# A decoder step on one core: output and gate-path weights split once into a DRAM copy, and fetched ready-made

## The chip, the core and the metric

The kernel runs on one core of a Trainium2 chip. The metric is the device time of one execution in microseconds (us). Five engines work side by side, each through its own instructions in a fixed order: the tensor engine (PE; its weight loads are listed apart as PEld), the vector engine (DVE), the scalar engine (ACT), GpSimd (POOL), and the sync engine (SP), which here only issues DMAs. An instruction that waits for a semaphore holds back all that stands behind it on its engine.

## What is computed

A layer of a hybrid decoder for 1024 prompt tokens and 8 single sample tokens with a cache. Cut to what matters here:

```python
q, ckv, skv, wkv, gl, za, u, zp = split(rmsnorm(x) @ w_in)
o_a = nsa_attention(q, gl, ckv, skv, wkv, ...)      # 3 branches, gated, 8 heads
o_p = pool_mixer(u, ...)                            # windows 2, 4, 8, 16
mix = concat([o_a * silu(za), o_p * silu(zp)])
y = rmsnorm(x + mix @ w_out)
```

The 512 columns `za` of `w_in` (the gate path of the attention group) and the 1024 x 1024 matrix `w_out` are the weights that the change is about.

## The kernel before, in words

Float32 products are made from float32r pieces: a matrix is split into a high part (`hi`, a rounded copy) and a low part (`lo`, the rest), and three matmuls (hi by hi, hi by lo, lo by hi) are summed. `split_w` (line 142) makes the pair from a raw tile: ACT copies, and DVE or GpSimd subtracts.

The stages in the order of the program: projection of the K/V columns; compression of the cache blocks and the `q` columns, with `q` written to DRAM (`q_d`); the pooling stage, a loop over 4 channel groups `g` (lines 798 to 856), each with a `u` and a `zp` weight tile through `load_tile` (line 387) and `feat_unit` (line 400), with the one-token attention `decode()` (line 548) woven between; then the prompt's attention in 32 units (query block `i`, head pair `j`, line 1148), and the end.

`decode()` has higher priority and works in a memory pool `dp`, which is closed at line 718. The pools that are opened after that on the same side (`at`, the attention's tiles) take over its addresses.

A unit of the attention has two halves. `stage1` (line 739) makes scores on PE (`S`, line 773, from a `qt` tile that `load_q` fetched from `q_d`), adds masks on DVE (line 736), takes the exponential on ACT (line 786) and scales on GpSimd (line 793), giving the tiles `Ps` and `Pw`. `stage2` (line 867) transposes those on PE (lines 883 and 891), splits them on ACT and DVE (lines 885 to 897) and multiplies by V (lines 902 to 909). `stage1` of the next unit runs among the steps of `stage2`.

Between the steps, `paced_fill` (line 1130) takes matmuls from a generator `filler` (line 1086). It gives first the `za` projection (`za_fill`, line 959: 4 weight tiles `pt` by 3 token chunks `c`, 24 matmuls each, lines 968 to 970), then the output projection (`out_half`, line 1069, matmuls at line 1042). `za_fill` loads and splits a weight tile with `load_tile`; after the last tile of each chunk it calls `load_wo(c)` (line 979), which puts split rows of `w_out` into the place of the input chunk that is no longer needed.

The framework's scheduler sets each engine's order at build time, by priority and by its own estimate of when an instruction is ready. Nothing is reordered on the chip.

Of the kernel before, what the change touches and what calls it, by code (L numbers as in the profile page):

```python
# [7 lines left out]
F32 = mybir.dt.float32  # L8
F32R = mybir.dt.float32r
I32 = mybir.dt.int32  # L10
BF16 = mybir.dt.bfloat16
AF = mybir.ActivationFunctionType
# [24 lines left out]
def r32(ap):  # L37
    return ap.bitcast(F32)
# [3 lines left out]
def hybrid_step_kernel(ctx, tc, xp, xs, ccmp, cslc, cwin, spool, ptab, norm_g, w_in, cmp_pe, cmp_w1,  # L42
# [17 lines left out]
    def ps_t(name="tp"):  # L60
        return psum.tile([128, 512], F32, name=name, tag="tp", bufs=3)
# [17 lines left out]
    b_d = dram.tile([4, 128, TOK], F32, name="b_d")  # L79
    g_d = dram.tile([NB, 24], F32, name="g_d")  # L80
    kc_d = dram.tile([2, 128, 128], F32, name="kc_d")


    ident = pers.tile([128, 128], F32, name="ident")
# [57 lines left out]
    def split_w(hi, lo, raw, eng=None):  # L142
        nc.scalar.activation(hi, raw, AF.Copy)
        (eng or nc.vector).tensor_sub(lo, raw, r32(hi))
# [252 lines left out]
    def w_cols(c0):  # L397
        return w_in.rearrange("(k p) c -> p k c", p=128)[:, :, c0:c0 + 128]
# [10 lines left out]
    def silu2(out, src):  # L409

        nc.scalar.activation(out, src, AF.Tanh, scale=0.5)
        nc.vector.scalar_tensor_tensor(out, out, 1.0, src, op0=OP.add, op1=OP.mult)
# [305 lines left out]
    des.close()  # L718


    at = ctx.enter_context(tc.tile_pool(name="at", bufs=2, reuse_waits="tile"))
    UNITS = [(i, j) for i in range(8) for j in range(4)]
    q_tiles = {}
    soft = {}
# [73 lines left out]
    for g in range(4):  # L798
        w = 2 << g
        hi, lo = load_tile(w_cols(C_U + g * 128))  # L800
        u = pu.tile([128, H0 + TOK], F32, name="u", bufs=2)
        nc.vector.memset(u[:, :H0], 0.0)
        for c in range(3):
            p, t0, n = feat_unit(hi, lo, c)
            nc.scalar.activation(u[:, H0 + t0:H0 + t0 + n], p[:, :n], AF.Copy)
        p = ps_t("ut")
        nc.tensor.transpose(p[:15, :128], u[:, H0 + T - 15:H0 + T], ident)
        nc.tensor.transpose(p[:NB, 128:256], u[:, H0 + T:H0 + TOK], ident)
        nc.tensor.transpose(p[:, 256:376], spt[:, g * 128:(g + 1) * 128], ident[:120, :120])
        nc.vector.tensor_copy(utok[:15, g * 128:(g + 1) * 128], p[:15, :128])  # L810
        nc.vector.tensor_copy(utoks[:, g * 128:(g + 1) * 128], p[:NB, 128:256])
        us = pp.tile([128, NB, 16], F32, name="us", bufs=2)
        nc.vector.tensor_copy(us[:, :, :15], p[:, 256:376].rearrange("p (b s) -> p b s", b=NB))
        nc.vector.tensor_copy(us[:, :, 15], u[:, H0 + T:H0 + TOK])
        cur = u
        step = 1
        k = 0
        while step < w:
            nx = pp.tile([128, H0 + TOK], F32, name=f"ws{k % 2}")
            nc.vector.memset(nx[:, :H0], 0.0)  # L820
            nc.vector.tensor_add(nx[:, H0:H0 + T], cur[:, H0:H0 + T], cur[:, H0 - step:H0 + T - step])
            cur = nx
            step *= 2
            k += 1
        nc.vector.tensor_reduce(cur[:, H0 + T:H0 + TOK], us[:, :, 16 - w:], axis=AX.X, op=OP.add)
        nc.vector.scalar_tensor_tensor(cur[:, H0:H0 + w - 1], cur[:, H0:H0 + w - 1], float(w),
                                       cnt[:, :w - 1], op0=OP.mult, op1=OP.mult)
        dd = cur[:, H0:]
        nc.vector.scalar_tensor_tensor(dd, dd, 1.0 / w, u[:, H0:], op0=OP.mult, op1=OP.subtract)
        if g == 2:  # L830
            load_q(0, 0)
            load_q(0, 1)
        if g == 3:
            for _ in stage1(*UNITS[0]):
                pass
        hi, lo = load_tile(w_cols(C_ZP + g * 128))
        sz = pu.tile([128, TOK], F32, name="sz")
        for c in range(3):
            p, t0, n = feat_unit(hi, lo, c)
            silu2(sz[:, t0:t0 + n], p[:, :n])  # L840
        if g:
            bb = pp.tile([128, TOK], F32, name="bb")
        for c in range(3):
            t0, n = CHUNKS[c]
            p = ps_t("yp")
            nc.tensor.matmul(p[:, :n], pw[:, g, :], dd[:, t0:t0 + n], start=True, stop=True)
            cs = slice(t0, t0 + n)
            if c < 2:
                nc.vector.scalar_tensor_tensor(bb[:, cs], p[:, :n], psc[:, g:g + 1], sz[:, cs],
                                               op0=OP.mult, op1=OP.mult)  # L850
            else:

                nc.scalar.activation(bb[:, cs], p[:, :n], AF.Copy, scale=psc[:, g:g + 1])
                nc.gpsimd.tensor_mul(bb[:, cs], bb[:, cs], sz[:, cs])
                nc.gpsimd.tensor_copy(bs_t[:, g, :], bb[:, T:])
        nc.gpsimd.dma_start(b_d[g], bb)
    tc.keep_in_program_order(nc.sync.dma_start(npool_p, utok[:15]))
    tc.keep_in_program_order(nc.sync.dma_start(npool_s[:, 14], utoks))
    pes.close()


# [97 lines left out]
    def za_fill():  # L959
        w = {}  # L960
        for pt, c in ZORD:
            if pt not in w:
                w[pt] = load_tile(w_cols(C_ZA + pt * 128))
            hi, lo = w[pt]
            for t0, n in CHUNKS[c:c + 1]:
                p = ps_j()
                for k in range(8):
                    nc.tensor.matmul(p[:, :n], hi[:, k, :], xh[c][:, k, :], start=k == 0, stop=False)  # L968
                    nc.tensor.matmul(p[:, :n], hi[:, k, :], xl[c][:, k, :], start=False, stop=False)  # L969
                    nc.tensor.matmul(p[:, :n], lo[:, k, :], xh[c][:, k, :], start=False, stop=k == 7)  # L970
                    if k == 7:
                        gate(pt, t0, n, p)
                    yield
            if pt == 3:
                with tc.high_priority(2000):
                    load_wo(c)
        xt_es.close()

    def load_wo(c):

        rows = WROWS[c]
        w = xtp.tile([128, 2, CHUNKS[c][1] * 8], F32R, name=f"wo{c}", tag=f"x{c}")
        w = w[:, :, :512 * len(rows)].rearrange("p f (k c) -> p f k c", c=512)
        for j in range(0, len(rows), 2):
            half, k = rows[j]
            raw = rp.tile([128, 2, 512], F32, name="wo_raw", tag="r")
            nc.sync.dma_start(raw, w_out[k * 128:(k + 2) * 128, half * 512:half * 512 + 512]
                              .rearrange("(k p) c -> p k c", p=128))
            for kk in range(2):
                nc.scalar.activation(w[:, 0, j + kk], raw[:, kk], AF.Copy)  # L990
                (nc.vector, nc.gpsimd)[kk].tensor_sub(w[:, 1, j + kk], raw[:, kk], r32(w[:, 0, j + kk]))
                O_[half, k + kk] = w[:, 0, j + kk], w[:, 1, j + kk]

    def open_out():
        fp, op = (ctx.enter_context(tc.tile_pool(name=n, bufs=1, side="right", reuse_waits="tile"))
# [275 lines left out]
```

## Time and profile before

| what | value |
|---|---|
| median of 3 runs | 641.39 us (641.33 to 641.68) |
| the profiled execution's own time | 641.35 us |
| its span, first to last instruction | 639.7 us |
| PE busy | 625.0 us, 4176 matmuls |
| PEld busy | 581.1 us |
| DVE busy | 420.9 us |
| ACT busy | 364.1 us |
| POOL busy | 270.2 us |
| share of the chain that ended last | PE 90%, DVE 4%, issue 2% |

The profiled execution takes 1.65 us more than its span, for what lies around the instructions. Busy time of PE counts modelled ends of pipelined matmuls, so small gaps can hide in it.

### The profile page before, as it was taken

How to read it: one execution, taken by the hardware profiler on the slowest of the kernel's cores; microseconds unless marked ns; L12 is line 12 of the kernel's file. 1: busy time of each engine (PE TensorE's matmuls, PEld its weight loads, DVE VectorE, ACT ScalarE, POOL GpSimd, SP SyncE). 2: the span in 40 equal slices, each digit the busy share in tenths (PEclk: the TensorE clock that was granted, in tenths of full speed). 3: DMA queues.
4: the chain of work that ended last, by engine and by line, in shares of the span. 5: the costliest groups of instructions: out<-in, count | busy, mean ns of one | idle time of the engine just before them, and what ended most of it. 6: DMA issues, size and time to landing. Idle time of an engine off the chain costs nothing.

```text
span 639.7 us, 12220 instructions
## 1 busy us (share of the span) xinstructions
PE 625.0 (98%) x4176; PEld 581.1 (91%) x4176; DVE 420.9 (66%) x1237; ACT 364.1 (57%) x931; POOL 270.2 (42%) x412
## 2 busy tenths in 40 slices
PE   8999999999999999999999999999999999999995
PEld 5999999999999899999899999788899999998895
DVE  6754234637264547466787999778888787877653
ACT  5654223536223333218787988767686767676742
POOL 6144004404035624006546767544545555444510
PEclk9999999999999999999999999999999999999998
DMA  8435107956234532243313456403113020101001
GB/s 281 151 91 156 34 1 223 287 199 193 61 80 135 158 98 87 84 119 93 91 34 99 121 189 184 118 18 100 37 50 98 17 100 17 67 17 67 17 34 66
DMA packets 63741, 65.13 MB, mean 102 GB/s; under 512 B 4487, under 2 KB 55119, under 8 KB 63639
## 3 DMA queue, kind: packets, MB, share of 16 engines
q1 hardware_dynamic: 53631, 44.55, 23.0%
q0 software_dynamic: 4000, 12.76, 6.3%
q10 hardware_dynamic: 6048, 7.05, 3.2%
q8 instruction: 33, 0.54, 0.3%
q14 instruction: 29, 0.24, 0.1%
HBM read 50.98 MB, written 15.68 MB: 104 GB/s over the span
## 4 chain that ended last, share of the span: by engine, by line
PE 90%; DVE 4%; issue 2%; DMA 1%; ACT 1%; POOL 1%; DVEq 0%; POOLq 0%; ACTq 0%
PE pj L1042 14%; PE S L773 9%; PE tp L891 8%; PE pa L404 7%; PE pa L405 7%; PE pa L406 7%; PE O L909 5%; PE O L908 4%; PE pa L277 4%; PE pa L275 3%; PE pa L276 3%; PE pj L968 2%; PE pj L969 2%; PE pj L970 2%; PE xtp_ps L230 1%
## 5 line engine op out<-in xcount | busy, mean ns | idle before, releaser
L793 POOL TENSOR_SCALAR Ps<-Ps,sm,gates 128x64 f32<-128x64 f32 (+1 forms) x120 | 76.4, 647 | 87.5 <-DVE sm L789 57.9
L897 DVE TENSOR_TENSOR pl<-tp,ph 128x512 fp32r<-128x512 f32 (+1 forms) x136 | 89.9, 670 | 21.2 <-ACT ph L896 19.9
L773 PE MATMUL S<-KT,qt 128*128 128x320 f32 (+10 forms) x400 | 99.5, 347 | 3.1 <-DVE sm L736 3.1
L896 ACT ACTIVATE ph<-tp 128x512 fp32r<-128x512 f32 (+1 forms) x136 | 77.1, 580 | 31.4 <-PE tp L891 21.5
L404 PE MATMUL pa<-x,ws_hi 128*128 128x384 f32 (+1 forms) x288 | 93.7, 325 | 0.0
L406 PE MATMUL pa<-x,ws_lo 128*128 128x384 f32 (+1 forms) x288 | 92.9, 323 | 0.0
L405 PE MATMUL pa<-x,ws_hi 128*128 128x384 f32 (+1 forms) x288 | 92.7, 322 | 0.0
L786 ACT ACTIVATE Ps<-Ps,sm 128x64 f32<-128x64 f32 (+8 forms) x128 | 71.0, 555 | 24.5 <-DVE sm L736 22.5
L1042 PE MATMUL pj<-wo,mh 128*128 128x512 f32 (+1 forms) x272 | 84.5, 385 | 0.0
L909 PE MATMUL O<-pl,V 128*128 128x256 f32 x264 | 76.5, 308 | 0.2
L908 PE MATMUL O<-ph,V 128*128 128x256 f32 x264 | 74.5, 298 | 0.0
L773 PEld LDWEIGHTS S<-KT,qt 128*128 128x128 f32 x400 | 63.2, 189 | 9.0 <-DVE sm L736 3.5
L1042 PEld LDWEIGHTS pj<-wo,mh 128*128 128x128 f32 x272 | 48.4, 188 | 6.9 <-DVE r L1054 0.3
L405 PEld LDWEIGHTS pa<-x,ws_hi 128*128 128x128 f32 x288 | 54.2, 188 | 0.4 <-issue 0.3
L404 PEld LDWEIGHTS pa<-x,ws_hi 128*128 128x128 f32 x288 | 54.2, 188 | 0.4
L406 PEld LDWEIGHTS pa<-x,ws_lo 128*128 128x128 f32 x288 | 54.2, 188 | 0.2
L277 PE MATMUL pa<-w_hi,x 128*128 128x256 f32 (+1 forms) x184 | 52.9, 288 | 1.2 <-DVE x L236 1.2
L275 PE MATMUL pa<-w_hi,x 128*128 128x256 f32 (+1 forms) x184 | 53.6, 292 | 0.0
L909 PEld LDWEIGHTS O<-pl,V 128*128 128x128 f32 x264 | 49.8, 189 | 2.9 <-DVE pl L897 0.6
L276 PE MATMUL pa<-w_lo,x 128*128 128x256 f32 (+1 forms) x184 | 52.4, 285 | 0.0
L1042 PE MATMUL pj<-wo,ml 128*128 128x512 f32 (+1 forms) x136 | 51.7, 380 | 0.0
L908 PEld LDWEIGHTS O<-ph,V 128*128 128x128 f32 x264 | 49.9, 189 | 1.8
(294 smaller groups left out, 1530.5 us busy)
## 6 DMA issues: line engine op xcount, KB each, us to landing
ws_raw<-in_w_in SPq DMA_DIRECT2D x32, 256.0 KB, 3.0
qt<-q_d SPq DMA_DIRECT2D x64, 128.0 KB, 2.9
x_t<-in_x_prompt SPq DMA_DIRECT2D x8, 512.0 KB
wo_raw<-in_w_out SPq DMA_DIRECT2D x8, 512.0 KB, 3.8
r<-in_x_prompt SPq DMA_DIRECT2D x8, 512.0 KB, 3.2
out<-r SPq DMA_DIRECT2D x7, 512.0 KB, 2.9
q_d<-qhl ACTq DMA_DIRECT2D x8, 384.0 KB, 3.9
out<-kvf ACTq DMA_DIRECT2D x5, 512.0 KB, 3.1
```

The lines of the kernel that those rows point to most:

```text
L275: nc.tensor.matmul(p[:n, :cn], xh[c][:, k, ts_], hi[:, k, :cn], start=k == 0, stop=False)
L277: nc.tensor.matmul(p[:n, :cn], xl[c][:, k, ts_], hi[:, k, :cn], start=False, stop=k == 7)
L404: nc.tensor.matmul(p[:, :n], hi[:, k, :], xh[c][:, k, :], start=k == 0, stop=False)
L405: nc.tensor.matmul(p[:, :n], hi[:, k, :], xl[c][:, k, :], start=False, stop=False)
L406: nc.tensor.matmul(p[:, :n], lo[:, k, :], xh[c][:, k, :], start=False, stop=k == 7)
L773: nc.tensor.matmul(S[:, :ln], qt[:, f, h, :], KT[:, kv, k0 + a:k0 + a + ln], start=f == 0, stop=f == 1)
L793: nc.gpsimd.tensor_scalar(regs[br], regs[br], sm[:, hh, 2, br:br + 1], gsrc[:, k:k + 1], op0=OP.mult, op1=OP.mult)
L896: nc.scalar.activation(ph[:, :m], tp[:, :m], AF.Copy)
L897: nc.vector.tensor_sub(pl[:, :m], tp[:, :m], r32(ph[:, :m]))
L908: nc.tensor.matmul(O[:, :256], vv, ph[:, a * 256:(a + 1) * 256], start=False, stop=False)
L909: nc.tensor.matmul(O[:, :256], vv, pl[:, a * 256:(a + 1) * 256], start=False, stop=last)
L1042: nc.tensor.matmul(p, a[:, k % 4, :], w, start=first and kk == 0, stop=last and kk == 2)
```

## The change

Two DRAM tensors are added: `zw_d` for the split gate-path weights and `wo_d` for the split output weights. The pooling loop now calls `stage_some(3)` at two places in each of its 4 rounds, which makes 24 tiles in all: 8 of gate-path weights and 16 of output weights. For one tile SP loads 256 KB into `sraw`, ACT copies the high part into half of `sw`, GpSimd subtracts into the other half, and a DMA from GpSimd's queue writes the 512 KB of `sw` to DRAM. `sraw` and `sw` have two buffers each, in a pool `stg` that is opened right behind `at`, in memory that `decode()` had. `za_fill` and `load_wo` then fetch the split tiles from SP's queue and no longer split anything.

```diff
+    zw_d = dram.tile([4, 2, 128, 1024], F32, name="zw_d")
+    wo_d = dram.tile([2, 8, 128, 2, 512], F32, name="wo_d")
...
+    ses = ExitStack()
+    to_stage = [(zw_d[pt, :, :, kk * 128:(kk + 4) * 128].rearrange("f p c -> p f c"),
+                 w_cols(C_ZA + pt * 128)[:, kk:kk + 4], 4) for pt in range(4) for kk in (0, 4)]
+    to_stage += [(wo_d[half, k], w_out[k * 128:(k + 1) * 128, half * 512:half * 512 + 512], 1)
+                 for rows in WROWS for half, k in rows]
+
+    def stage_some(n):
+        for dst, src, k in to_stage[:n]:
+            raw = stg.tile([128, 512], F32, name="sraw", bufs=2)
+            nc.sync.dma_start(raw.rearrange("p (k c) -> p k c", k=k) if k > 1 else raw, src)
+            w = stg.tile([128, 2, 512], F32R, name="sw", bufs=2)
+            split_w(w[:, 0], w[:, 1], raw, nc.gpsimd)
+            nc.gpsimd.dma_start(dst, r32(w))
+        del to_stage[:n]
+
     at = ctx.enter_context(tc.tile_pool(name="at", bufs=2, reuse_waits="tile"))
+    stg = ses.enter_context(tc.tile_pool(name="stg", bufs=1, reuse_waits="tile"))
...
             nc.scalar.activation(u[:, H0 + t0:H0 + t0 + n], p[:, :n], AF.Copy)
+        stage_some(3)
...
             silu2(sz[:, t0:t0 + n], p[:, :n])
+        stage_some(3)
...
+    ses.close()
     pes.close()
...
-                w[pt] = load_tile(w_cols(C_ZA + pt * 128))
+                w[pt] = [ws.tile([128, 8, 128], F32R, name=n, bufs=2) for n in ("ws_hi", "ws_lo")]
+                for f in range(2):
+                    nc.sync.dma_start(r32(w[pt][f].rearrange("p k c -> p (k c)")), zw_d[pt, f])
...
-        for j in range(0, len(rows), 2):
-            half, k = rows[j]
-            raw = rp.tile([128, 2, 512], F32, name="wo_raw", tag="r")
-            nc.sync.dma_start(raw, w_out[k * 128:(k + 2) * 128, half * 512:half * 512 + 512]
-                              .rearrange("(k p) c -> p k c", p=128))
-            for kk in range(2):
-                nc.scalar.activation(w[:, 0, j + kk], raw[:, kk], AF.Copy)
-                (nc.vector, nc.gpsimd)[kk].tensor_sub(w[:, 1, j + kk], raw[:, kk], r32(w[:, 0, j + kk]))
-                O_[half, k + kk] = w[:, 0, j + kk], w[:, 1, j + kk]
+        for j, (half, k) in enumerate(rows):
+            nc.sync.dma_start(r32(w[:, :, j]), wo_d[half, k])
+            O_[half, k] = w[:, 0, j], w[:, 1, j]
```

The order that the scheduler made of it is shown at three places. Lines in the rows of the changed kernel are its own: 143 has become 145, 411 is 413, 853 is 874, 786 is 805, 732 is 751.

On ACT, at the end of the pooling stage, there stood before (`sz` is the gate of the last group, `ws_hi` the first two copies for `za_fill`, `bb` the last pooling output, `Ps` and `Pw` the first exponentials of the attention):

```order
L411 ACTIVATE sz<-pa 128x384
L143 ACTIVATE ws_hi<-ws_raw 128x512 x2
L411 ACTIVATE sz<-pa 128x264
L853 ACTIVATE bb<-yp,psc 128x264
L786 ACTIVATE Ps,sm<-Ps,sm 128x64
L786 ACTIVATE Ps,sm<-Ps,sm 128x128
L786 ACTIVATE Pw,sm<-Pw,sm 128x128
```

and now:

```order
L413 ACTIVATE sz<-pa 128x384
L413 ACTIVATE sz<-pa 128x264
L145 ACTIVATE sw<-sraw 128x512 x2
L874 ACTIVATE bb<-yp,psc 128x264
L145 ACTIVATE sw<-sraw 128x512 x13
L805 ACTIVATE Ps,sm<-Ps,sm 128x64
L805 ACTIVATE Ps,sm<-Ps,sm 128x128
L805 ACTIVATE Pw,sm<-Pw,sm 128x128
```

The copies of 15 of the 24 tiles stand behind the last `sz` and ahead of the first exponential. From the third on, each waits in the built program for its own load and for the DMA that wrote the tile two before it. The first load of `sraw` waits for PE and GpSimd instructions of `decode()`.

Further on ACT, among the first units' exponentials, stand the other 9 copies (`pc` and `ph` are the first transposed blocks of the attention, `zt` the first gate of `za_fill`):

```order
L145 ACTIVATE sw<-sraw 128x512
L805 ACTIVATE Ps,sm<-Ps,sm 128x128
L805 ACTIVATE Pw,sm<-Pw,sm 128x128 x2
L145 ACTIVATE sw<-sraw 128x512 x6
L907 ACTIVATE pc<-tp 64x256
L918 ACTIVATE ph<-tp 128x512
L907 ACTIVATE pc<-tp 64x256
L145 ACTIVATE sw<-sraw 128x512
L962 ACTIVATE zt<-pj 128x384
```

GpSimd has the subtractions and writes in the same order: 15 ahead of its first scaling of the attention, the 16th after nine scalings, the 17th after three more, and after six more, which end the third unit, the last 7 in one piece ahead of the fourth unit's first scaling.

On SP, at the same point, the order was (`qt` are the query tiles of the attention, eight DMAs for the four pairs of one query block):

```order
L393 DMA ws_raw<-in_w_in 128x4x128 x12
L857 DMA out<-utok 15x512
L858 DMA out<-utok 8x512
L732 DMA qt<-q_d 64x4x128 x16
L393 DMA ws_raw<-in_w_in 128x4x128 x2
```

and is now:

```order
L732 DMA sraw<-in_w_in 128x4x128 x4
L987 DMA ws_hi<-zw_d 128x1024
L987 DMA ws_lo<-zw_d 128x1024
L732 DMA sraw<-in_w_in 128x4x128 x3
L987 DMA ws_hi<-zw_d 128x1024
L987 DMA ws_lo<-zw_d 128x1024
L732 DMA sraw<-in_w_in 128x4x128
L732 DMA sraw<-in_w_out 128x512 x7
L751 DMA qt<-q_d 64x4x128 x8
L732 DMA sraw<-in_w_out 128x512 x2
L751 DMA qt<-q_d 64x4x128 x8
L732 DMA sraw<-in_w_out 128x512 x7
```

The first query tiles have moved behind 15 of the staging loads, of which each from the third on waits for the subtraction two tiles before. On PE the first 24 `za` matmuls still stand ahead of the first score. Counted in the order, 72 `za` matmuls, 38 scores and the V products of two units (10 matmuls) stood ahead of the fourth unit's first transpose (line 883); now 24, 38 and those of one unit (5).

## Rows read from the trace of the kernel before

**Rows 1.** Chain that ended last, shares by engine, from the page.

```profile
PE 90%; DVE 4%; issue 2%; DMA 1%; ACT 1%; POOL 1%; DVEq 0%; POOLq 0%; ACTq 0%
```

**Rows 2.** Busy time by stretch: start, end, length, engines, then clock, DMA share, GB/s.

```profile
core 0: us, PE busy (x) PEld busy (x) DVE busy (x) ACT busy (x) POOL busy (x), PEclk, DMA share, GB/s
99.00:160.00 61.00, 61.00 (x394) 60.34 (x393) 34.80 (x80) 28.41 (x57) 21.66 (x28) 1.00 0.75 231
160.00:284.00 124.00, 123.02 (x781) 116.72 (x780) 65.26 (x170) 38.37 (x90) 36.67 (x51) 1.00 0.36 104
284.00:402.00 118.00, 114.29 (x799) 107.39 (x798) 97.51 (x379) 96.31 (x306) 74.95 (x129) 1.00 0.36 114
402.00:633.00 231.00, 230.76 (x1480) 206.58 (x1478) 173.60 (x517) 154.52 (x369) 106.97 (x152) 1.00 0.17 54
633.00:640.00 7.00, 0.00 (x0) 0.00 (x0) 1.94 (x7) 1.47 (x4) 0.00 (x0) 0.73 0.20 76
```

**Rows 3.** Groups of instructions, those that the change removes.

```profile
L144 DVE TENSOR_TENSOR ws_lo<-ws_raw,ws_hi 128x512 fp32r<-128x512 f32 x40 | 28.2, 729 | 25.4 <-ACT ws_hi L143 25.2
L991 POOL TENSOR_TENSOR wo<-wo_raw,wo 128x512 fp32r<-128x512 f32 x8 | 11.4, 1424 | 1.8 <-ACT wo L990 1.6
L991 DVE TENSOR_TENSOR wo<-wo_raw,wo 128x512 fp32r<-128x512 f32 x8 | 9.8, 1230 | 0.0
L990 ACT ACTIVATE wo<-wo_raw 128x512 fp32r<-128x512 f32 x16 | 9.2, 627 | 0.0
```

**Rows 4.** Timeline of ACT at the end of the pooling stage.

```profile
281.17 1.15 ACT L143 ACTIVATE ws_hi<-ws_raw 128x512 fp32r<-128x512 f32 x2 [2.36 <-PE pa L405]
282.22 0.37 ACT L411 ACTIVATE sz<-pa 128x264 f32<-128x264 f32 x1
...
288.30 0.35 ACT L786 ACTIVATE Ps<-Ps,sm 128x64 f32<-128x64 f32 x1 [4.40 <-DVE sm L736]
```

**Rows 5.** Timeline of POOL there: last pooling product, scalings 1 and 9.

```profile
285.01 0.75 POOL L854 TENSOR_TENSOR bb<-bb,sz 128x264 f32<-128x264 f32 x1 [27.17 <-DVE sz L412]
...
289.98 0.40 POOL L793 TENSOR_SCALAR Ps<-Ps,sm,vgate 128x64 f32<-128x64 f32 x1 [3.33 <-DVE sm L736]
...
293.47 0.45 POOL L793 TENSOR_SCALAR Pw<-Pw,sm,gates 128x128 f32<-128x128 f32 x1
```

**Rows 6.** DMA issues: KB each, median us from issue to landing.

```profile
qt<-q_d SPq DMA_DIRECT2D x64, 128.0 KB, 2.9
...
q_d<-qhl ACTq DMA_DIRECT2D x8, 384.0 KB, 3.9
...
b_d<-bb POOLq DMA_DIRECT2D x4, 516.0 KB, 3.0
...
q_d<-qhl ACTq DMA_DIRECT2D x4, 256.0 KB, 6.1
```

**Rows 7.** Instructions on the tensor b_d: ns min/median/max, first and last start.

```profile
L856 POOL DMA_DIRECT2D b_d<-bb x4: 570/583/630, 201.3 to 286.1; - x4
```

**Rows 8.** Timeline of SP's queue: one weight load, and the first query tiles.

```profile
180.15 0.37 SPq L393 DMA_DIRECT2D ws_raw<-in_w_in  x1
...
273.18 19.80 SPq L732 DMA_DIRECT2D qt<-q_d  x16
```

**Rows 9.** Timeline of PE: first gate-path matmul, first scores.

```profile
282.98 0.53 PE L968 MATMUL pj<-x,ws_hi 128*128 128x384 f32 x1
...
287.36 0.81 PE L773 MATMUL S<-KT,qt 128*128 128x192 f32 x6
288.57 1.95 PE L773 MATMUL S<-KT,qt 128*128 128x128 f32 x12 [0.41 <-DVE sm L736]
```

**Rows 10.** Timeline of PE: gate-path matmuls of the third chunk, fourth unit's transpose.

```profile
298.58 0.28 PE L970 MATMUL pj<-x,ws_lo 128*128 128x264 f32 x1
298.70 0.28 PE L968 MATMUL pj<-x,ws_hi 128*128 128x264 f32 x1
...
303.54 0.27 PE L883 MATMUL tp<-ident,Ps 128*64 128x128 f32 x1
```

## The prediction

> **What bounds the kernel now.** I read the chain that ended last first: 90% of it is PE [rows 1]. Then the busy time by stretch [rows 2]. From 402 to 633 us PE is busy for 230.76 of 231 us: there only PE work counts. From 284 to 402 us, where the first half of the attention is interleaved with the gate-path projection and the output weights are split, PE is busy for 114.29 of 118 us, with DVE (97.51) and ACT (96.31) not far below. So the work that the change takes away lies in the one later stretch that isn't wholly PE's. From 160 to 284 us, the pooling stage with the one-token attention woven in, PE is full too (123.02 of 124), but POOL has 87 us free and ACT 86. That is where the 24 tiles would cost nothing. The question is whether they get there.
>
> **What is taken away.** On ACT 16 copies of the output weights at 0.63 us and the last copies of the gate path, on DVE 8 subtractions at 1.23 and some at 0.73, on POOL 8 at 1.42 [rows 3]. PE gains from that only what it loses in 284 to 402. At least, that is its idle time, 118 - 114.3 = 3.7 us. At most it is the time without a weight load, 118 - 107.4 = 10.6, since back-to-back matmuls could hide further gaps [rows 2]. The saturated stretch behind it has 11% without a weight load as well, so much of the 10.6 is no loss. I take 5, nearer to the lower end.
>
> **What is added, and where it stands.** One tile costs ACT a copy of 0.63 us and POOL a subtraction of 1.42 [rows 3] and a DMA issue of 0.58 [rows 7]. By busy time 24 tiles are 48 us of POOL and 15 of ACT, which would fit before 284. But the order puts them elsewhere. The staging buffers lie where the one-token attention worked, whose PE work ends at the end of the stage, and the first two copies stand on ACT behind the last gate of the pooling stage, `sz`, which ran at 282.22 [rows 4]. So nothing of the staging begins before about 281. From there it doesn't lie beside other work, it stands in front of it: 15 copies ahead of the first exponential on ACT, 15 subtractions ahead of the first scaling on POOL, 15 loads ahead of the first query tile on SP. PE has only what comes before the first score, the first 24 gate matmuls, and those too wait now for a tile that must go to DRAM and back.
>
> **The pace of the staging.** With two `sw` buffers, tile n+2 can be copied only when the write of tile n has landed. A buffer's round is copy 0.63, subtraction 1.42, issue to landing of the write, and about 0.1 for the hand-overs (an estimate). The trace has no 512 KB write under this load. The `b_d` write of 516 KB from POOL landed in 3.0 us in a stage that moved 104 GB/s; the `q_d` writes landed in 3.9 (384 KB) and 6.1 (256 KB) in the stage that moved 231 GB/s at a DMA share of 0.75 [rows 2, 6]. The staging moves 768 KB per tile, some 260 GB/s at 3 us a tile, so its nearest row is the loaded one whose size is nearest, 3.9. The round is then 6.05 us and the pace c = 3.0 us per tile. The ends are 3.0 (c = 2.6) and 6.1 (c = 4.1).
>
> **The clock of the changed kernel, worked out.**
> - Without the two `ws_hi` copies of 1.15 us in front of it, the last `sz` ends about 281.8 [rows 4], copies 1 and 2 by 283.0. POOL's two subtractions end at 285.3. The pooling product of 0.75 that stands next [rows 5] takes it to 286.1, where write 1 is issued. It lands at 290.0, and copy 3 begins.
> - Copy 15 begins at 290.0 + 12 x 3.0 = 326.0.
> - SP's load 15 waits for subtraction 13, at 290.0 + 10 x 3.0 + 2.15 = 322.2. With that load and the four issues of the first query tile at 0.37 [rows 8] and 2.9 to landing [rows 6], the first score is at 327.0. Before, it was 0.94 us from the first score (287.36) to the first exponential (288.30) [rows 4, 9]. So that one comes at 327.9, which is 39.6 later.
> - First scaling 1.68 later, as before (288.30 to 289.98), 329.6; nine of them take 3.94 [rows 4, 5], to 333.5. Subtraction 16 and three scalings (1.3) go to 336.2, when write 16 is issued; it lands at 340.1. There copy 18 begins, and copy 24 begins 6 x 3.0 later, at 358.1, and ends at 358.7.
> - Behind copy 24 on ACT stand a gate and a block copy (about 0.5 each, an estimate from the 0.63 of a copy), then the fourth unit's exponentials, and 1.68 later its scaling: 361.5. PE transposes it 0.4 later, at 361.9, against 303.54 before [rows 10]. PE is **58.4 us late**.
>
> **What PE still owes at that point.** By the order, 48 gate matmuls and one unit's five V products fewer are done by then. 24 matmuls of the first chunks took 287.36 - 282.98 = 4.4 us [rows 9]; 24 of the third chunk at 0.12 (298.58 to 298.70 [rows 10]) are 2.9; the five V products are like those, 0.6. Together **7.8 us**.
>
> **The restart.** While it waits PE has about 10 us of work in 78. The clock fell to a mean of 0.73 in the last 7 us, where PE has nothing left [rows 2], so it will be at 1.2 GHz in the gap and come back some time after. Also the gate matmuls that covered the latencies of the first units are not between them. [...]
>
> **The sum.** 58.4 + 7.8 - 5 + 4 = 65.2 us. From the fourth unit on the program is as before, and PE-bound. 641.35 of the profiled execution plus 65.2 is 706.6, and I say **707 us**. The median of the runs, 641.39, is the same within the spread of the runs; 0.2% of it, 1.3 us, is about what a measurement of this kernel can tell from no change.
>
> **Rivals.**
> - *Writes queue behind reads.* The DMA engines are near full during the staging, and the writes land like the slowest row, 6.1. The landing counts half in each of 18 intervals and whole at the start and at write 16, so 11 times: 11 x 2.2 = 24 us more, 731. For it: 260 GB/s asked for, more than the 231 of the stage with that row. Against: its median for larger writes is 3.9. The Trainium skill, page "DMA: Bandwidth & Descriptors", section "Latency and other measured facts", says that the access latency of DRAM rises from 0.2 us on average to 2 us at high load, and that it dominates a DMA's fixed cost. No run here shows that latency by itself; by it the write would land in 3.0 + 1.8 = 4.8 us and the sum would be 717.
> - *The staging runs at POOL's own pace.* If the landings are covered, a tile costs POOL 1.42 + 0.58 = 2.0 us, and 18 intervals take 18 us less: 689. Against: with two buffers that needs a landing of 1.9 us, and the `b_d` writes took 3.0 [rows 6]; other small gains would have to add up to it.
> - *Not slower.* The staging runs where its code stands, in the pooling stage, and the later stretch gives back 3.7 to 10.6 us: 631 to 638. For it: 87 us of free POOL time there [rows 2]. Against: ACT's order has the first copy behind the last `sz`, and no engine reorders. It decides from the point where the first exponential is late by less than the 10.6 that can come back, which one tile ahead of it would allow, and fifteen don't.
>
> **Chances.** The forecast with c between 2.6 and 3.4 (697 to 717) 0.73; the queued writes 0.12; the short staging 0.11; not slower 0.04, half of it within 0.2%. The range reaches from the short staging's upper part to most of the way to the queued writes: 690 to 727. Faster by over 0.2% has 0.02, within 0.2% 0.02, slower 0.96.
>
> **What would show it.** In the changed profile, the copies of the staging on ACT should start at 281 to 284, come in pairs every 6 us, and each wait for a DMA of `zw_d` or `wo_d`. The first exponential should be at 322 to 335, with query tiles landing just before it. PE should be nearly empty between 287 and 355 except for a few us of gate matmuls and scores, with a lowered clock; from about 365 it should be full to the end, about 335 us long. DVE and ACT should have less to do in the stretch that has the gate path. Wrong would be: staging copies before 275; a pace far from 3 us; or a first exponential before 300.

## The result, and the profile after

The changed kernel takes **722.02 us** (median of 5 runs, 721.40 to 725.19), the kernel before 641.44 on the same chip (641.33 to 642.86). The ratio is 1.127, with a 95% interval of 1.124 to 1.129. The forecast was 707 us in a range of 690 to 727: the mechanism came as forecast, and its main term was too small. 722 lies above the 697 to 717 that the forecast's own pace covered; it is inside the range because that reached on towards the queued writes' 731.

The profiled execution, one of 723.86 us, spans 722.2 us, 82.5 more than the 639.7 before. The chain that ended last, by engine, is the first thing to read beside [rows 1]:

```profile
PE 75%; DMA 16%; POOL 3%; ACT 2%; issue 2%; SPq 1%; DVE 1%; ACTq 0%; POOLq 0%; DVEq 0%
```

DMA went from 1% to 16% of the chain. The busy time by stretch says where (columns as in [rows 2]):

```profile
99.00:160.00 61.00, 61.00 (x395) 60.24 (x394) 34.07 (x82) 27.58 (x55) 22.18 (x28) 1.00 0.76 233
160.00:284.00 124.00, 122.94 (x781) 116.86 (x780) 65.25 (x168) 37.76 (x89) 37.12 (x52) 1.00 0.30 88
284.00:402.00 118.00, 46.58 (x256) 43.03 (x255) 29.94 (x156) 46.67 (x154) 68.70 (x102) 0.67 0.67 219
402.00:700.00 298.00, 292.86 (x1925) 268.54 (x1924) 221.19 (x707) 204.87 (x512) 140.10 (x214) 0.99 0.29 90
700.00:715.00 15.00, 15.00 (x105) 13.87 (x104) 8.05 (x17) 5.38 (x15) 1.40 (x4) 1.00 0.09 36
```

Up to 284 us nothing changed. From 284 to 402 PE works 46.58 us where it worked 114.29, at a mean granted clock of 0.67 (the clock that PE was given, as a share of 2.4 GHz), while the DMA engines go from a share of 0.36 to 0.67. From 402 on PE is full again but for 5 us. POOL did no more from 160 to 284 than before, 37.12 against 36.67 us: no tile got into the pooling stage.

ACT's timeline shows the queue itself. Start and duration come first; in brackets stand the idle time ahead and what ended it. The first row holds copies 1 and 2, the others are copies 3 to 7, 9, 15, 18 and 24 of the staging, and the first exponential:

```profile
283.00 1.14 ACT L145 ACTIVATE sw<-sraw 128x512 fp32r<-128x512 f32 x2
290.72 0.63 ACT L145 ACTIVATE sw<-sraw 128x512 fp32r<-128x512 f32 x1 [5.74 <-DMA zw_d<-sw]
292.14 0.63 ACT L145 ACTIVATE sw<-sraw 128x512 fp32r<-128x512 f32 x1 [0.79 <-DMA zw_d<-sw]
301.48 0.63 ACT L145 ACTIVATE sw<-sraw 128x512 fp32r<-128x512 f32 x1 [8.71 <-DMA sraw<-in_w_in]
302.69 0.63 ACT L145 ACTIVATE sw<-sraw 128x512 fp32r<-128x512 f32 x1 [0.58 <-DMA sraw<-in_w_in]
310.59 0.63 ACT L145 ACTIVATE sw<-sraw 128x512 fp32r<-128x512 f32 x1 [7.26 <-DMA zw_d<-sw]
...
316.74 0.63 ACT L145 ACTIVATE sw<-sraw 128x512 fp32r<-128x512 f32 x1 [2.79 <-DMA zw_d<-sw]
...
336.08 0.63 ACT L145 ACTIVATE sw<-sraw 128x512 fp32r<-128x512 f32 x1 [2.83 <-DMA wo_d<-sw]
340.50 0.35 ACT L805 ACTIVATE Ps<-Ps,sm 128x64 f32<-128x64 f32 x1 [3.79 <-DVE sm L755]
...
351.62 0.63 ACT L145 ACTIVATE sw<-sraw 128x512 fp32r<-128x512 f32 x1 [3.36 <-DMA wo_d<-sw]
...
372.47 0.63 ACT L145 ACTIVATE sw<-sraw 128x512 fp32r<-128x512 f32 x1 [2.43 <-DMA wo_d<-sw]
```

Fifteen copies stand ahead of the first exponential, which comes at 340.50 and not at 288.30 [rows 4]. Of the 22 copies from the third on, 17 wait for a written tile to land, and three for a raw tile. Two things in these rows were not forecast. Copy 5 waits 8.71 us, and what comes last for it is a raw tile, not a write. And the pace differs: copies 3 to 9 need 26.0 / 6 = 4.3 us each, copies 9 to 15 need 19.3 / 6 = 3.2, copies 18 to 24 need 20.9 / 6 = 3.5.

SP's queue shows what stands between those tiles (rows as in [rows 8]):

```profile
276.21 10.38 SPq L732 DMA_DIRECT2D sraw<-in_w_in  x4
292.13 0.34 SPq L987 DMA_DIRECT2D ws_hi<-zw_d  x1
292.52 0.50 SPq L987 DMA_DIRECT2D ws_lo<-zw_d  x1
293.13 10.74 SPq L732 DMA_DIRECT2D sraw<-in_w_in  x3
```

The read-back of the first gate weights, 1 MB in two reads, stands on the same queue as the raw loads, and it is issued only when its tiles have been written. That wait itself cost the fifth raw tile little: its buffer came free at 292.69, when the third subtraction ended (291.43 + 1.26), and it is asked for at 293.13. What is late is the landing. This is the row of the DMA issues for 292 to 307 us alone, which holds the four gate writes that were issued within 3 us of a pair of read-backs:

```profile
zw_d<-sw POOLq DMA_DIRECT2D x4, 512.0 KB, 6.9
```

They landed in 6.6 to 7.4 us; the two gate writes before them took 3.8 and 4.4, the two behind them 3.8 and 4.1. The third write, issued at 292.99, landed at 300.4, one microsecond before copy 5, and the raw tile later still. So copies 3 to 9 are slow because what they wait for lands late.

PE's rows show the effect (idle time and its releaser in brackets), and two stretches the clock (columns as in [rows 2]):

```profile
296.21 0.66 PE L992 MATMUL pj<-x,ws_hi 128*128 128x384 f32 x1 [11.80 <-DMA ws_hi<-zw_d]
...
302.12 0.52 PE L994 MATMUL pj<-x,ws_lo 128*128 128x384 f32 x1
302.44 0.40 PE L992 MATMUL pj<-x,ws_hi 128*128 128x384 f32 x1
302.68 0.34 PE L993 MATMUL pj<-x,ws_hi 128*128 128x384 f32 x1
302.86 0.34 PE L994 MATMUL pj<-x,ws_lo 128*128 128x384 f32 x1
...
337.32 0.93 PE L792 MATMUL S<-KT,qt 128*128 128x192 f32 x3 [33.08 <-DMA qt<-q_d]
...
369.80 0.58 PE L924 MATMUL O<-pc,Vc 128*128 128x256 f32 x1 [21.86 <-DVE pc L908]
...
376.67 0.27 PE L905 MATMUL tp<-ident,Ps 128*64 128x128 f32 x1
...
490.87 1.22 PE L792 MATMUL S<-KT,qt 128*128 128x352 f32 x3 [4.79 <-DMA qt<-q_d]
```

```profile
297.00:302.00 5.00, 4.08 (x13) 3.89 (x13) 0.00 (x0) 0.52 (x1) 0.00 (x0) 0.50 0.91 322
302.50:304.00 1.50, 1.50 (x10) 1.42 (x8) 0.00 (x0) 0.63 (x1) 1.20 (x2) 0.98 0.00 0
```

Three gaps of 11.80, 33.08 and 21.86 us, 66.7 in all, hold most of the loss. The gate matmuls between the first two take 0.52 us each and start 0.32 apart at a granted clock of 0.50 (297 to 302 us), which is 1.2 GHz; behind 302.5, at 0.98, which is 2.4 GHz, they take 0.34 and start 0.18 apart. PE had been idle for 11.8 us before them. The fourth unit's transpose, at 303.54 before [rows 10], comes at 376.67. The last row is a wait that wasn't there before and that I hadn't forecast.

The DMA issues of after (columns as in [rows 6]):

```profile
wo_d<-sw POOLq DMA_DIRECT2D x16, 512.0 KB, 4.1
qt<-q_d SPq DMA_DIRECT2D x64, 128.0 KB, 4.6
wo<-wo_d SPq DMA_DIRECT2D x16, 512.0 KB, 7.6
...
zw_d<-sw POOLq DMA_DIRECT2D x8, 512.0 KB, 5.5
```

### The profile page after: what moved, and what is told of

The parts are those of the page before. It is cut to its first block, busy times and chain, and to the rows that moved or that the text cites. A ratio compares the mean times of both kernels' runs of the same rounds, so it can differ in the third digit from the quotient of the medians.

```text
span 722.2 us, 12332 instructions
## 1 busy us (share of the span) xinstructions
PE 633.5 (88%) x4176; PEld 591.1 (82%) x4176; DVE 408.3 (57%) x1221; ACT 368.6 (51%) x931; POOL 299.1 (41%) x452
## 2 busy tenths in 40 slices
DMA packets 72830, 90.31 MB, mean 125 GB/s; under 512 B 5383, under 2 KB 56015, under 8 KB 72727
## 4 chain that ended last, share of the span: by engine, by line
PE 75%; DMA 16%; POOL 3%; ACT 2%; issue 2%; SPq 1%; DVE 1%; ACTq 0%; POOLq 0%; DVEq 0%
PE pj L1060 12%; PE S L792 8%; PE tp L913 7%; PE pa L406 6%; PE pa L408 6%; PE pa L407 6%; DMA wo_d<-sw 5%; DMA qt<-q_d 4%; PE O L931 4%; PE O L930 4%; PE pa L279 2%; PE pa L277 2%; DMA zw_d<-sw 2%; PE pa L278 2%; PE pj L992 1%
## 5 line engine op out<-in xcount | busy, mean ns | idle before, releaser
L792 PE MATMUL S<-KT,qt 128*128 128x320 f32 (+10 forms) x400 | 104.2, 364 | 41.6 <-DMA qt<-q_d 39.7
L812 POOL TENSOR_SCALAR Ps<-Ps,sm,gates 128x64 f32<-128x64 f32 (+1 forms) x120 | 73.4, 623 | 122.5 <-DVE sm L808 101.3
L792 PEld LDWEIGHTS S<-KT,qt 128*128 128x128 f32 x400 | 68.4, 205 | 47.0 <-ACT sw L145 33.4
L755 DVE CUSTOM_DVE_ANT_0 Ps<-S,mc 128x64 f32<-128x64 f32 x64 | 14.1, 220 | 71.4 <-PE S L792 64.8
L146 POOL TENSOR_TENSOR sw<-sraw,sw 128x512 fp32r<-128x512 f32 x24 | 30.2, 1260 | 53.4 <-ACT sw L145 53.3
L805 ACT ACTIVATE Pw<-Pw,sm 128x640 f32<-128x640 f32 (+4 forms) x64 | 44.3, 692 | 15.5 <-DVE sm L755 14.9
```

Of the source, the lines that this page charges most:

```text
L792: nc.tensor.matmul(S[:, :ln], qt[:, f, h, :], KT[:, kv, k0 + a:k0 + a + ln], start=f == 0, stop=f == 1)
L805: e = nc.scalar.activation(regs[br], regs[br], AF.Exp, scale=-1.0, bias=sm[:, hh, 0, br:br + 1], accum_out=sm[:, hh, 1, br:br + 1])
L812: nc.gpsimd.tensor_scalar(regs[br], regs[br], sm[:, hh, 2, br:br + 1], gsrc[:, k:k + 1], op0=OP.mult, op1=OP.mult)
```

## The experiments

**The theory** is place and pace: the tiles stand in in-order queues (ACT, POOL, SP) ahead of the attention's first units, each costs what a two-buffer round with a DRAM write in it takes, and PE can do little meanwhile. **The rival** is traffic: the change moves 25.2 MB more through the DMA engines (90.31 MB against 65.13), and those cost their 82 us wherever they stand. A third reading is that the gate path's return trip through DRAM alone is the loss.

**No staging at all** (the upper bound of the gain):

```diff
-        stage_some(3)
...
-                    nc.sync.dma_start(..., zw_d[pt, f])
+                    nc.sync.dma_start(..., q_d[f, pt * 128:(pt + 1) * 128])
...
-            nc.sync.dma_start(r32(w[:, :, j]), wo_d[half, k])
+            nc.sync.dma_start(r32(w[:, :, j]), q_d[half, ...])
```

> No tile is staged: the split is left out, and where the changed kernel fetches ready gate-path and output weights, this one fetches rows of the same shape and size from the queries' DRAM tensor q_d, so its gate and output weights are other data. It bounds what the fetch of ready tiles can gain. Theory (place and pace: the loss is the in-order queue of 24 tiles that stands ahead of the first units of the attention): with no tile there, the first exponential comes at 285 to 292 us as before (288.3), PE has no gap, and 3.7 to 10.6 us come back, less up to 4.8 for the new wait for query tiles at 486 us if it stays: 632 to 643 us. Rival (traffic: the 25.2 MB more that the DMA engines move cost their 82 us wherever they stand, 3.3 us per MB): the doubled fetches alone are 6.3 MB more, 641 + 21 = 662 us.

It took 644.6 us, a ratio of 1.0034 (1.002 to 1.005): 1.6 us above the theory's upper end, and far from the rival's 662. The first exponential is at 289.17 us. The windows of this kernel in the two stretches that matter:

```profile
360.00:402.00 42.00, 42.00 (x323) 40.93 (x322) 37.44 (x141) 35.34 (x97) 23.09 (x41) 1.00 0.59 188
402.00:440.00 38.00, 30.89 (x195) 26.43 (x193) 23.01 (x79) 20.67 (x50) 12.38 (x18) 0.91 0.46 119
```

From 360 to 402 PE is full, where it was idle for 2.2 us before. Behind it PE loses 7.1 us, so that PE would have no gap was wrong. The wait is this row of PE's timeline, for a block of the pooling result that stands in SP's queue behind the output weights and two cache copies (the caches' copies from DRAM to DRAM, one of them 2 MB):

```profile
412.54 1.22 PE L1058 MATMUL pj<-wo,mh 128*128 128x512 f32 x2 [6.62 <-ACT mh L1038]
```

So even free tiles gained nothing here: what PE got back it lost again in a queue.

**Gate path alone, output weights alone.** The first kernel stages the 8 gate tiles and splits the output weights late, the second the reverse:

```diff
-    to_stage += [(wo_d[half, k], w_out[...], 1) for rows in WROWS for half, k in rows]
```

> Only the 8 tiles of the gate-path weights are staged and fetched ready; the output weights are split late, as before the change. Theory (place and pace): by ACT's order only 2 copies stand ahead of the first exponential and the query tiles are loaded behind two raw tiles, so the first exponential is within 6 us of 288.3; the other 6 tiles stand between the first units, in 3 pairs of some 7 us each that partly lie beside the units: 645 to 662 us. Rival (traffic): a third of the tiles, a third of the loss, 641 + 27 = 668 us. A third reading, that the loss is the gate path waiting for its tiles to come back from DRAM, has all of the loss here: above 690 us.

> Only the 16 tiles of the output weights are staged and fetched ready; the gate path's weights are split where they are used, as before the change. Theory (place and pace): ACT's order has 15 copies ahead of the first exponential, as in the changed kernel; with no tile read back amid them the pace is 3.2 us per tile (what copies 9 to 15 showed in the changed kernel): first exponential at 282.7 + 7 + 13 x 3.2 = 331 us, 43 us late, and as only one tile stands between the units afterwards, 641 + 43 + 0 to 12 = 684 to 696 us. Rival (traffic): two thirds of the loss, 696 us; it does not say where. The gate path waiting for its tiles: 641 us, no loss.

Output weights alone: 700.9 us, 1.091 (1.088 to 1.095). Copies 3 to 15 run from 294.41 to 333.18 us, 3.23 us each, as expected; the first exponential is at 336.19, 5 us later than I had put it, since copy 3 had to wait for the first write until 294.41 and not until 290. The time is 5 us above the 684 to 696 that I expected. No gate tile goes through DRAM here, so the third reading is out. The time is also near the rival's 696, so this run doesn't decide against traffic.

Gate path alone: 671.4 us, 1.046 (1.043 to 1.049). My 645 to 662 was a miss, and the rival's 668 came nearer. The first exponential is as early as said, at 284.11. The loss lies behind it, and DVE's timeline names the largest part of it:

```profile
328.48 0.58 DVE L938 TENSOR_TENSOR za<-O,ol 64x128 f32<-64x128 f32 x2 [11.37 <-DMA zw_d<-sw]
```

`za` is allocated where the staging buffers lay (bytes 97472 to 113984 of each partition against 97472 to 109760). So the first attention output can't be written before the last staged tile has left for DRAM. It left at 324.25 and landed 3.96 later, at 328.21. PE waited for this 12.7 us of the 29 that were lost; the rest is in smaller waits and in a granted clock of 0.63 from 290 to 306 us, while the DMA engines were at a share of 1.01. In the changed kernel the same memory is shared, but the wait ends together with the queue: its first `za` is written at 378.93, 0.3 us after write 24 landed.

**All 24 tiles early.** The same instructions and bytes, placed between the token tiles of the key and value stage, with three buffers of each kind:

```diff
+    stg = ses.enter_context(tc.tile_pool(name="stg", ..., side="right", ...))
     for br in range(2):
...
+            stage_some(2)
...
+    ses.close()
     ws = xt_es.enter_context(tc.tile_pool(name="ws", ...))
```

> All 24 tiles are staged, written and fetched as in the changed kernel, the same instructions and bytes, but between the token tiles of the key and value stage (42 to 99 us), where POOL is busy 11 of 57 us, ACT 20 and the DMA engines move some 75 GB/s; the buffers (3 and 3) lie in memory that is free there. Theory (place and pace): no tile stands ahead of the first exponential any more, which comes within 10 us of 288.3; the 18.9 MB of 24 tiles need 65 us at 290 GB/s, so the last few tiles run into the compression stage and hold its loads up by some us: 633 to 655 us. Rival (traffic): the bytes are the same, 715 to 725 us.

684.3 us, 1.066 (1.062 to 1.069): half of the loss gone with the same traffic, which the rival forbids, but far above the theory's 655. The first exponential, expected within 10 us of 288.3, came at 313.79. Its windows show what took the place of the old gap:

```profile
60.00:80.00 20.00, 19.33 (x159) 19.05 (x158) 5.11 (x12) 9.32 (x23) 12.79 (x15) 1.00 0.89 287
80.00:99.00 19.00, 17.42 (x132) 16.67 (x131) 9.33 (x20) 8.48 (x26) 12.66 (x14) 1.00 0.87 302
99.00:115.00 16.00, 4.08 (x32) 3.63 (x31) 6.28 (x23) 6.62 (x14) 12.01 (x16) 0.72 0.95 321
115.00:130.00 15.00, 5.38 (x17) 2.84 (x17) 10.22 (x12) 7.66 (x13) 12.27 (x13) 0.50 0.99 335
```

Here the DMA engines are the limit. The tiles that don't fit before 99 us meet the compression stage's loads, which alone took a share of 0.75 [rows 2], and PE stands 12.3 us for one of those:

```profile
115.39 0.69 PE L497 MATMUL z_ps<-ident,pr 128*128 128x128 f32 x2 [12.31 <-DMA pr<-out]
```

So traffic does cost here, where the DMA engines were already busy.

**The pace.** One kernel stages all tiles as the change does but fetches the gate tiles from older data (the first edit of `dma_start` above, alone), the other leaves the line with the write out and fetches all tiles from older data:

> All 24 tiles are staged and written as in the changed kernel, but the gate path fetches its 8 tiles from q_d, which was written long before: same size, other data, so the gate is not the reference's. The read-backs on SP then wait for no staged tile. Theory (the read-backs, left out of the prediction, slowed the first tiles from 3.2 to 4.3 us): in the changed kernel they wait on SP for a written tile to land, and the raw loads behind them wait too. Here copies 3 to 9 go at 3.2 us as well, some 6.5 us earlier in all, and the first 24 gate matmuls run at 283 as before the change: first exponential at 333 to 336 us, 712 to 717 us in all. Rival (the DMA engines' load sets the pace: the bytes are the same): first exponential at 340 us, 720 to 724 us.

> All 24 tiles are loaded, copied and subtracted in the changed kernel's order, but not written to DRAM: the 24 write issues on POOL and 12.6 MB are left out, and the ready tiles are fetched from q_d (other data). Theory (a buffer's round with the landing in it sets the pace): without the write a raw buffer's round is left, landing 2.9 + copy 0.63 + subtraction 1.25 = 4.8 us for two tiles, 2.4 us a tile: first exponential at 283 + 13 x 2.4 = 314 us, and the whole 722 - 24 x (3.65 - 2.4) = 692 us. Rival (the order alone, the engines' own work and the loads): if the pace stays above 3.3 us the time stays above 715 us.

Without the return trip: 717.4 us, 1.117 (1.115 to 1.120), 0.4 above the theory's 717 and under the rival's 720. Copies 3 to 15 run from 289.60 to 327.67, 3.17 us each, and the first exponential is at 332.38, about as the theory said. Gate writes 3 to 6, which took 6.9 us in the changed kernel, land as fast as the others (the row for 291 to 302 us):

```profile
zw_d<-sw POOLq DMA_DIRECT2D x4, 512.0 KB, 4.1
```

The read-backs are issued at 266 and 281 us here, ahead of all the writes, so the run takes both the wait on SP and the 2 MB of reads out of this stretch. It shows what the return trip costs; by the issue times of the changed kernel the cost is in the landings, and not in the order on SP that the theory named.

Without the write: 698.9 us, copies 3 to 15 from 287.60 to 317.01, 2.45 us each (2.4 expected). The first exponential came at 320.61, 6 us later than expected, and the whole 7 us later, but the rival's 715 is out. With the rows of the changed kernel, where 17 of 22 copies wait for a write, this says that the landing in the buffer's round sets the pace. What this run doesn't separate is the wait for the writes from the 12.6 MB that they move; a kernel with three buffers of each kind in the same place would help there, and was not run.

**The wait at 486 us.**

```diff
-        if x == 14:
+        if x == 20:
             tc.keep_in_program_order(nc.sync.dma_start(nwin_s[:, 0:255], cwin[:, 1:256]))
```

> The changed kernel with one thing moved: the two cache copies on SP's queue (2 MB in one of them) stand behind the 21st unit of the attention and not behind the 15th, away from the ready output weights' 8 MB. Theory (the wait of 4.8 us for query tiles at 486 us comes from that queue, where a query tile stands behind the copy and the output weights' reads): the wait goes, 717 to 719 us. Rival (the ready output weights' reads alone hold the query tiles up): 721 to 723 us.

721.1 us, 1.122 (1.121 to 1.124): a little below the changed kernel, and in the rival's 721 to 723. The wait didn't go: it shrank to 3.35 us and moved to 497.5, where the query tiles stand behind four output-weight reads and other loads. The copies were at most a part of it.

**Versions that fit.** Fewer tiles early, and the late splitting kept for the others; all but the first also move the cache copies, and the third stages nothing.

> The 8 gate-path tiles alone are staged, between every second token tile of the key and value stage, the output weights split late as before the change. 8 tiles are 6.3 MB, which the 42 to 99 us stretch has room for (75 of some 290 GB/s used). Theory (place: what costs is the queue ahead of the attention, and in the run with all tiles early the 14 tiles that were still to be written after 86 us, when the compression stage's loads began): nothing collides, first exponential at 284 to 290 us, and the relief of DVE and ACT in the stretch from 284 to 402 us is a third to a half of 3.7 to 10.6: 637 to 642 us. Rival (traffic wherever it stands): 641 + 27 = 668 us.

> 14 tiles, the 8 of the gate path and the 6 of the first block of the output weights, are staged between the token tiles of the key and value stage, one after each; the other 10 output tiles are split late as before the change. The two cache copies on SP's queue move from the 15th to the 21st unit of the attention, away from the output weights' loads. Theory (place): 14 tiles are 10.7 MB, at 2.65 us each 37 us, so they end before 99 us, where the compression stage starts; no loss there beyond 3 us, and 4 to 5 us back between 284 and 412 us: 635 to 642 us. Rival (traffic): 641 + 48 = 689 us.

> The kernel that stages nothing and fetches ready tiles from q_d (split left out, gate and output weights are other data), with the two cache copies moved from the 15th to the 21st unit. It bounds what ready tiles can gain at all. In the run without the move 4.9 us came back before 402 us and 7.1 were lost at 402 to 412 us, where PE waited 6.6 us for a block of b_d behind 5 MB of output weights and copies. Theory (that wait is the queue's, as in the changed kernel's wait at 486 us): it goes, 634 to 639 us. Rival (the doubled reads of the output weights are themselves too slow): 641 to 645 us.

> 12 tiles staged between the token tiles of the key and value stage, 8 of the gate path and 4 of the output weights' first block, the other 12 output tiles split late as before the change; cache copies behind the 21st unit. With 14 tiles PE lost 5 us from 60 to 130 us, 2.7 of them behind loads that started late after the last tiles, and got 3.6 back from 284 to 402. Theory: two tiles fewer end 5 us earlier, the loss before 160 us is 1 to 3 us, the relief 3 to 4: 637 to 642 us. Rival: the loss stays (the q stage's weight loads wait for the staging's memory, however many tiles): 642 to 645 us.

> The 8 gate-path tiles staged in the key and value stage, output weights split late as before the change, and the cache copies moved from the 15th to the 21st unit. With 8 tiles and the copies in their old place PE lost 3.9 us from 360 to 402 us, where it lost 2.2 before the change. Theory (copies and output weights in one queue): the loss goes to 1 us or less: 637 to 641 us. Rival (ACT's splitting of the output weights is what PE waits for there): 641 to 644 us.

| tiles early | cache copies | median us | ratio (95%) | PE busy of 118 us, 284 to 402 |
|---|---|---|---|---|
| 8, gate | 15th unit | 642.97 | 1.0021 (1.0002 to 1.0039) | 113.97 |
| 14 | 21st | 642.58 | 1.0015 (0.9996 to 1.0034) | 117.89 |
| 12 | 21st | 642.52 | 1.0012 (0.9994 to 1.003) | 116.17 |
| 8, gate | 21st | 639.02 | 0.995 (0.9937 to 0.9963) | 115.46 |
| none, data free | 21st | 638.78 | 0.9951 (0.9935 to 0.9967) | 117.71 |

Eight tiles, 6.3 MB, cost 1.3 us (0.2%) and not the rival's 27: **traffic by itself is refuted**, though the 637 to 642 that I expected was missed by 1 us as well. With 14 tiles PE gets 3.6 us back and loses 5.1 from 60 to 130 us, where it was busy throughout before. With 12 it gets 1.9 back and loses 2.0 from 60 to 160. Both come out at no change, half a microsecond above their expected ranges; for the 12 tiles the loss was as expected, and the relief of 3 to 4 wasn't. In the last row the copies' move took the loss at 402 to 440 from 7.1 to 2.3 us, about as the theory said. That row is also the most that ready tiles gave in any run, 0.5%, and only together with the moved copies: without the move the same kernel was 0.3% slower than before.

The 8-tile version with the copies moved is 0.5% faster than the kernel before; without the move it gained nothing. The expectation that its loss from 360 to 402 us would go to 1 us failed: it is 2.4 us (3.9 without the move, 2.2 before the change). Whether the moved copies alone would bring the kernel before the same gain was not run and stays open.

## Why the prediction was right, and where it was off

**The place: right.** No copy started before 275 us; the first began at 283.0, where 281.8 was worked out. The POOL time that is free in the pooling stage stayed free, because the buffers lie in the one-token attention's memory and ACT and POOL ran in the built order. SP's waits from 230 to 320 us show what the first staging load stood for, a matmul of `decode()` (L732 is the load of `sraw`; then who it waits for, us in total, times, longest):

```profile
SPq L732 <- PE dO L686: 37.1, 1, 37.1
```

The kernels with 8 tiles before and at that place (643 against 671 us) bear it out, though they also differ in three buffers against two. Staging in the pooling stage with buffers in other memory was not run.

**The pace: right in kind, mis-sized.** The forecast was 3.0 us per tile; the trace shows 4.3, 3.2 and 3.5. Copy 15 began at 336.1 and not at 326.0, copy 24 at 372.5 and not at 358.1: 14.4 us. The first exponential, which was to come at 322 to 335, came at 340.5. These 14.4 us are nearly all of the error of the 58.4 us term, which measured 73.1 (376.67 against 303.54 before). Of them 0.7 lie before copy 3, 8.0 between copies 3 and 9, 1.3 from there to copy 15, 1.4 to copy 18 and 2.9 to copy 24. Three things make them up:
- The return trip of the gate tiles, which the step left out: it put 15 loads ahead of the first query tile on SP, but not the four read-backs between them, beside which four writes took about 7 us to land. Without them the first exponential came 8.1 us earlier (332.4 against 340.5).
- The round without them: landing 4.1 + copy 0.63 + subtraction 1.26 + 0.3 from there to the write's issue + 0.1 = 6.4 us, 3.2 per tile. The forecast had a landing of 3.9, a subtraction of 1.42, and only 0.1 for the hand-overs.
- Tiles between the first units, at 3.5 each: there copies and subtractions stand behind exponentials and scalings too. The 17th write was issued only at 352.67, behind six scalings.

**The queued writes (0.12), the nearest rival.** Its mechanism was there for four of the 24 writes, the gate writes beside the read-backs, which passed its 6.1 (6.6 to 7.4); the others stayed under 5, and the output tiles' median is 4.1. So the measured 722 lies between the forecast and this rival's 731, and the median of all gate writes, 5.5, hides two groups. The Trainium skill, page "DMA: Bandwidth & Descriptors", section "Latency and other measured facts", gave by its rise of the latency at high load an estimated 4.8 us and 717. The measured landings, 4.1 and 6.9, lie on both sides of it. The nearest row of before, 3.9, was close for the output tiles.

**POOL's pace (0.11).** Even without writes the pace was 2.45 us, set by the raw loads; POOL's 2.0 was never reached.

**What came after the fourth unit.** Forecast 7.8 - 5 + 4 = 6.8 us; measured 345.53 - 336.16 = 9.4 us from its transpose to the end. In it is the new wait of 4.8 us at 486, which "from the fourth unit on the program is as before" had ruled out. The relief of 5 is neither confirmed nor refuted. With no staging and the copies moved PE was busy 117.7 - 114.3 = 3.4 us longer in that stretch; but its profiled execution was 4.4 us shorter although it lost 2.3 from 402 to 440, which makes 6.7, with the moved copies in it. No run shows the 4 us that the sum has for the restart. What the changed kernel's rows show is the clock's part of it:

```profile
377.90:381.00 3.10, 3.02 (x11) 2.53 (x11) 2.92 (x17) 2.71 (x11) 2.08 (x6) 0.50 0.34 94
381.00:402.00 21.00, 21.00 (x154) 20.69 (x154) 16.23 (x72) 17.23 (x62) 11.89 (x25) 1.00 0.36 101
```

Behind the fourth unit's transpose PE worked 3.0 us at a granted clock of 0.50, and from 381 on it was full at 1.00. The clock took about 1.5 us of that, an estimate: half of the 3.0, as the matmuls above start 0.32 us apart at the lower level and 0.18 at the higher. The owed work and the latencies were not measured apart.

## What to carry to other kernels

Work moved to where an engine has free time lands where its buffers' memory comes free, so look up which tile last held those bytes, and which tile takes them next: both were waits here. Spilling prepared data to DRAM puts a write's landing into a buffer's round, and that landing must be counted with all that moves at the same time, the read-backs of the same data included. Before moving work, bound the gain with a kernel that gets the data free: here it was 0.5% at most, and a queue collision elsewhere took all of it until two other copies were moved.

## What I had not expected of the hardware

The same four 512 KB writes landed in 4.1 us (median) without the read-backs amid them and in 6.9 beside them, with the same 90.31 MB moved in the whole kernel. A POOL subtraction and the write issued after it are 0.3 us apart (for the last tile the subtraction ends at 374.45, the issue is at 374.75). And with 24 tiles early the DMA engines moved 335 GB/s at a share of 0.99, more than the 287 of the busiest fortieth of the span before the change.
